# The second query up-projection tile and the transposes for the last residual, asked for at other places

## Chip, cores and metric

One NeuronCore of a Trainium2 chip runs the whole program. The metric is the device time of one execution in microseconds. A kernel is timed in several runs, and their median stands; one further execution is profiled.

## What is computed

Two transformer blocks over 256 tokens of width 1024, in float32. Two pieces of the reference matter here. In the first block's mixer, queries come out of a small projection:

```python
q = (rms_norm(c_q, g_cq) @ w_uq).reshape(B, L, MLA_HEADS, MLA_QK_DIM)   # 256 -> 8 heads x 96
q = rms_norm(q, g_q_mla)
```

In the second block, a layer of 16384 experts is added to the tokens h, and the result is normalised:

```python
u2 = rms_norm_2(h, norm2_g[l]) * (1 + sc2) + sh2
h = h + g2 * peer_layer(u2, peer_wq[l], peer_keys[l], peer_u[l], peer_v[l])
return rms_norm_2(h, final_g)
```

`peer_layer` projects the tokens to 8 heads of 2 x 128 queries, scores each half against 128 keys, chooses 16 pairs of keys for each head, and weighs expert activations.

## The kernel before

The work runs as one long stream of projections on TensorE. Tokens lie along the free dimension (256, with 16 meta tokens 272), features on the partitions, eight tiles of 128 for the width of 1024. A float32 product is made of three matmuls on rounded halves: high weight by high token, high by low, low by high (`mm3`, lines 118 to 121; a slice of 128 rows is three matmuls, a projection of 1024 rows 24).

**Weights.** `weights` (lines 89 to 108) loads one tile of 128 x 1024 on SP's queue (line 98), casts its high half on ScalarE (line 99, `whi`) and subtracts on VectorE, or on GpSimd where the call says so (line 100, `wlo`). Tiles of a name share buffers, given out in the order of use: three in the pool `w`, and in the first stages every fourth tile goes to a fourth buffer, `wx`. A cast can't start until the matmuls of the tile that had the buffer before are done.

**Order.** The program is written in plain Python order, and a planner sets the order of the instructions on each engine: the earliest in program order among what it believes ready. In `mixer` TensorE's order is the written one (`manual_schedule`), the other engines' is the planner's; in `experts` TensorE's is the planner's too. An engine works its list strictly in that order. SP's queue is such a list as well: a load that waits for a buffer holds up what stands behind it.

**Mixer, query up-projection** (lines 489 to 515). For each of two `w_uq` tiles g, four heads: six matmuls in a bank `sc`, a square on ScalarE (`qsq`), two multiplications on VectorE (`Q`, `qsw`). Behind a head follow a key's scaling (`scale_key`, from q = 2 on: two matmuls, then K's two multiplications on VectorE) and `step(1)`, half a projection of the `fq` or `fk` kind (`fox`): twelve matmuls. The second half of each calls `get_ready`, which requests the `w_in` tile of the next one. `fq` 0 to 3 use the `w_in` tiles 8 to 11; requests before are in this order: `w_in` 7, 8, `w_uq` 0, `w_in` 9, `w_in` 10, `w_uq` 1, `w_in` 11.

**Experts** (from line 1139). `raw` is the tokens times the gain, split in halves, slice k as soon as h[k] is final. Six query projections (line 1172, weights `peer_wq` 0 to 5) run on `raw` into six PSUM banks `mm`, while the sum of squares gives `r` (line 1178, in a bank `sc`, of which there are two, then a square root and a reciprocal). Then `affine` makes `u3` in eight slices (`aff` and `xl` on VectorE, `xh` on ScalarE) and `from_raw` (lines 781 to 788) multiplies a projection by `r` into `qt`, a tile named `pair`. `pair` has two buffers, shared by `qt` 0 and 1, the queries of later heads, and the transposed tokens. `scores` multiplies a head's queries with its keys in the banks `sc`. Projection 6 and later run on `u3`; projection 6 takes the bank of projection 0.

The tokens transposed, 16 transposes in four groups of four, each group in a bank `sc`, go through a copy (line 1165, to `pair`) and a store (line 1166) to `hd` in DRAM, which is read back near the end of the program. Once `h` is no longer read, its space goes to tiles of `experts`, the keys among them.

Of the kernel before, what the change touches and what calls it, by code (L numbers as in the profile page):

```python
# [10 lines left out]
F32 = mybir.dt.float32  # L11
# [12 lines left out]
S = 256  # L24
# [22 lines left out]
def two_blocks(ctx: ExitStack, tc: tile.TileContext, A, out):  # L47
    nc = tc.nc
    act, vec, pool, pe = nc.scalar, nc.vector, nc.gpsimd, nc.tensor
# [4 lines left out]
    ident = const.tile([128, 128], F32, name="ident")  # L54
# [5 lines left out]
    def col(name, k=0, p0=0, p1=128):  # L60
        o = COL[name][0] + k
        return cols[p0:p1, o:o + 1]

    xp = ctx.enter_context(tc.tile_pool(name="x", bufs=1))
    dram = ctx.enter_context(tc.tile_pool(name="hd", bufs=1, space=bass.MemoryType.DRAM))
# [18 lines left out]
    def bank(name):  # L84
        ids = banks[-1][name]
        ids.append(ids.pop(0))
        return ps.tile([128, 512], F32, name=name, tag=f"bank{ids[-1]}")
# [17 lines left out]
    def weights(*a, **kw):  # L105
        for w in weights_by_part(*a, **kw):
            pass
        return w
# [9 lines left out]
    def mm3(o, wh, wl, xh, xl, first, last):  # L118
        pe.matmul(o, lhsT=wh, rhs=xh, start=first, stop=False)  # L119
        pe.matmul(o, lhsT=wh, rhs=xl, start=False, stop=False)  # L120
        pe.matmul(o, lhsT=wl, rhs=xh, start=False, stop=last)  # L121
# [12 lines left out]
    def rstd_of(o, ssum, n):  # L134

        act.activation(o, ssum, AF.Sqrt, bias=eps[:o.shape[0]], scale=1.0 / n)
        vec.reciprocal(o, o)
# [36 lines left out]
    def split(p, x, T, nm, bufs=1):  # L174
        hi = p.tile([x.shape[0], T], F32R, name=nm + "h", bufs=bufs)
        lo = p.tile([x.shape[0], T], F32R, name=nm + "l", bufs=bufs)
        act.copy(hi, x)  # L177
        vec.tensor_sub(lo, x, hi)  # L178
        return hi, lo
# [4 lines left out]
    with psum(mm=8):  # L184
        o = bank("mm")
# [6 lines left out]
    for k in range(KC):  # L192
        if k % 4 < 2:
            first[k % 4] = next(loads[k % 4])
        t = hp.tile([128, T1], F32, name=f"h{k}")
# [60 lines left out]
    def mixer():  # L256
        es = ExitStack()
        p = es.enter_context(tc.tile_pool(name="mix", bufs=1))
# [48 lines left out]
        for c in range(2):  # L307
            t = p.tile([128, S], F32, name=f"cq{c}")
# [82 lines left out]
        for c in range(4):  # L391
            o = bank(("sc", "pm", "sc", "po")[c])
            cs = slice(c * 128, (c + 1) * 128)
            mm3(o[:, :T1], wkv[0][:, cs], wkv[1][:, cs], ckh, ckl, True, True)
            t = pw.tile([128, T1], F32, name="ksq", bufs=3)
# [12 lines left out]
        for i, t0 in enumerate((NM, NM + 128, 0)):  # L408
            o = bank("pm" if i == 1 else "sc")
            mm3(o, ckh[:, t0:t0 + 128], ckl[:, t0:t0 + 128], wkv[0][:, 512:], wkv[1][:, 512:], True, True)  # L410
            t = p.tile([128, 512], F32, name=f"V{i}")
# [73 lines left out]
        def sum_q(q0, q1):  # L485
            for q in range(q0, q1):
                pe.matmul(qsum[:8, :S], lhsT=sel[0:96, q], rhs=qsqs[q], start=False, stop=q == NH - 1)

        for g in range(2):
            wh, wl = weights(A["w_uq"][g])  # L490
            for q4 in range(4):
                q = 4 * g + q4
                o = bank("sc")
                for c in range(2):
                    cs = slice((q4 * 2 + c) * 128, (q4 * 2 + c + 1) * 128)
                    mm3(o[:, :S], wh[:, cs], wl[:, cs], cq3[c][0], cq3[c][1], c == 0, c == 1)
                t = pw.tile([96, S], F32, name="qsq", bufs=4)
                act.activation(t, o[0:96, :S], AF.Square)
                qsqs.append(t)
                qt = p.tile([96, S], F32, name=f"Q{q}")  # L500
                vec.scalar_tensor_tensor(qt, o[0:96, :S], col("gq", 0, 0, 96), rope[0:96, 0, NM:], op0=ALU.mult, op1=ALU.mult)
                t = pw.tile([96, S], F32, name="qsw")
                vec.scalar_tensor_tensor(t[64:96], o[96:128, :S], col("gq", 0, 96, 128), rope[96:128, 1, NM:], op0=ALU.mult, op1=ALU.mult)
                pool.tensor_add(qt[64:96], qt[64:96], t[64:96])
                Q.append(qt)
                if q == 1:
                    rfk = split(p, head_rstd(sum_fox("fk", T1), 64, T1, "rfk"), T1, "rfk")
                if q > 1:
                    scale_key(q - 2)
                step(1)  # L510
                if q > 4:
                    add_more(1)
                if q % 2 and q > 1:
                    sum_q(q - 3, q - 1)
# [164 lines left out]
        hx = [t[:, NM:] for t in h]  # L679
# [65 lines left out]
    def affine(p, xs, G, s0, r, T, nm, ks=range(KC)):  # L745

        res = []
        for k in ks:
            t = sm.tile([128, T], F32, name="aff")
            vec.scalar_tensor_tensor(t, xs[k], G[:, k:k + 1], r, op0=ALU.mult, op1=ALU.mult)  # L750
            hi = p.tile([128, T1], F32R, name=f"{nm}h{k}", bufs=1)[:, :T]
            lo = p.tile([128, T1], F32R, name=f"{nm}l{k}", bufs=1)[:, :T]
            sh = ada[:, s0 + k:s0 + k + 1]
            act.activation(hi, t, AF.Identity, bias=sh)
            vec.scalar_tensor_tensor(lo, t, sh, hi, op0=ALU.add, op1=ALU.subtract)  # L755
            res.append((hi, lo))
        return res
# [381 lines left out]
    def experts(hx):  # L1139
# [10 lines left out]
            return weights(ap, e=e, parts=parts, four=False, pin=pin)  # L1150

        qp = es.enter_context(tc.tile_pool(name="qp", bufs=2))
        qt = [qp.tile([128, 2, S], F32, name="pair") for n in range(2)]
        tc.keep_in_program_order(act.activation(dry, eps, AF.Sqrt))
        ss = sum_squares(sm, hx, S, vec)

        hd = dram.tile([128, 2, 1024], F32, name="hd")
        g2 = dram.tile([1, 1024], F32, name="g2")
        for i in range(2):
            for e2 in range(2):  # L1160
                o = bank("sc")
                for k in range(4):
                    pe.transpose(o[:, k * 128:(k + 1) * 128], hx[4 * e2 + k][:, i * 128:(i + 1) * 128], ident)
                t = qp.tile([128, 2, S], F32, name="pair").rearrange("p a b -> p (a b)")
                act.copy(t, o)
                nc.sync.dma_start(out=hd[:, i, e2 * 512:(e2 + 1) * 512], in_=t)
        vec.tensor_scalar(ada[:, 40:48], ada[:, 40:48], 1 / GATE, None, op0=ALU.mult)
        nc.sync.dma_start(out=g2.rearrange("a (k p) -> p (a k)", p=128), in_=ada[:, 40:48])
        G = gain_of(sm, 32, "norm2_g")
# [2 lines left out]
        for n in range(6):  # L1172
            o = bank("mm")
            project(o[:, :S + 2], wt(A["peer_wq"][n], vec if n == 1 else pool), raw, t1=S + 2)
            rp.append(o)
            if n == 0:
                o = bank("sc")
                tc.keep_in_program_order(pe.matmul(o[:, :S], lhsT=ones, rhs=ss, start=True, stop=True))
                r = qp.tile([128, S], F32, name="rstd", bufs=1)
                rstd_of(r, o[:, :S], 1024)  # L1180
        u3 = affine(xp, hx, G, 24, r, S, "x")
        rc = const.tile([128, 6], F32, name="rc")
        for n in range(4):
            from_raw(qt[n // 2][:, n % 2], rp[n], r, rc[:, n:n + 1])
# [2 lines left out]
        p = es.enter_context(tc.tile_pool(name="ex", bufs=1))  # L1187
# [178 lines left out]
        for m in range(KEYS // 2):  # L1366
# [10 lines left out]
            o = expert_acts(m, pool if m < OTHER else vec, OTHER <= m < DIRECT)  # L1377
            a = acts[:, 2 * m:2 * m + 2]
            if done:
                t = qp.tile([128, 2, S], F32, name="pair")  # L1380
# [43 lines left out]
        for i in range(2):  # L1424
            for n in range(3):
                add(ws[n], i, False, n == 2)
            for e2 in range(2):
                fs = slice(e2 * 512, (e2 + 1) * 512)
                t, x = part[:, 2 * i + e2], hf[:, i, fs]
# [13 lines left out]
    hx = [t[:, NM:] for t in h]  # L1443
# [147 lines left out]
```

## Time and profile before

| | us |
|---|---|
| median of 3 runs | 1692.92 |
| lowest and highest | 1692.71, 1694.39 |
| the profiled execution | 1697.36 |
| its span | 1695.6 |
| mean granted clock of TensorE in it | 0.99 |

The span is what the trace covers; the execution's time has 1.8 us more. Times in the trace are counted from the span's start. A matmul's start is recorded and its end is modelled, and matmuls overlap: intervals between starts tell the rate. PEclk is the share of full clock that was granted.

### The profile page before, as it was taken

To read this page: it belongs to the slowest core of one execution; us is meant where nothing else is said; L and a number is where in the kernel's file an instruction comes from. 1 tells how busy PE (TensorE), PEld (TensorE's weight loads), DVE (VectorE), ACT (ScalarE), POOL (GpSimd) and SP (SyncE) were. 2 spreads that over 40 slices of the span, in tenths; PEclk is the share of its full clock that TensorE was granted. 3 is DMA by queue.
4 is the path that set the end of the run, shared out by engine and by line. 5 is a ranking of instruction groups with operands and counts; after the bars stand their busy time and mean duration, and the time that the engine had idled before them with its cause. 6 is when DMAs were issued, how large, how long until landed. Compare 5 with 4: busy or idle time off the path is not lost.

```text
span 1695.6 us, 31038 instructions
## 1 busy us (share of the span) xinstructions
PE 1661.5 (98%) x11813; PEld 1539.0 (91%) x11813; DVE 1300.8 (77%) x2387; ACT 1015.3 (60%) x2037; POOL 133.4 (8%) x94
## 2 busy tenths in 40 slices
PE   9999999999999999999999989999999999999997
PEld 8999987799999888889989989999999988888886
DVE  8887677679875788886988997888889656666565
ACT  6544464664554776755664436988888555555554
POOL 3000002200000000000046920000000000000000
PEclk9999998999999999999999989999999999999999
DMA  7877642158786434336545545445454666655553
GB/s 264 287 235 251 204 149 88 38 199 275 259 265 177 160 133 141 134 113 209 177 155 171 175 138 173 161 163 169 164 165 162 194 232 196 195 191 198 189 197 125
DMA packets 90485, 308.20 MB, mean 182 GB/s; under 512 B 11352, under 2 KB 13912, under 8 KB 90208
## 3 DMA queue, kind: packets, MB, share of 16 engines
q1 hardware_dynamic: 90336, 306.22, 54.7%
q8 instruction: 93, 1.52, 0.4%
q14 instruction: 56, 0.46, 0.1%
HBM read 304.08 MB, written 2.10 MB: 181 GB/s over the span
## 4 chain that ended last, share of the span: by engine, by line
PE 85%; DVE 9%; ACT 4%; DMA 1%; issue 1%; SPq 0%; DVEq 0%; ACTq 0%
PE y L1407 20%; PE mm L119 17%; PE mm L121 17%; PE mm L120 17%; PE mm L824 5%; PE sc L1337 2%; DVE wlo L100 1%; ACT whi L99 1%; PE sc L548 1%; DMA wraw<-in_w_in_dram 1%; ACT tap L869 1%; DVE xl L755 1%; PE lev L978 1%; DVE acts L1252 1%; DVE acts L1250 0%
## 5 line engine op out<-in xcount | busy, mean ns | idle before, releaser
L99 ACT CAST whi<-wraw 128x1024 fp32r<-128x1024 f32 (+2 forms) x494 | 503.7, 1023 | 342.1 <-PE mm L120 230.7
L100 DVE TENSOR_TENSOR wlo<-wraw,whi 128x1024 fp32r<-128x1024 f32 (+2 forms) x457 | 545.3, 1197 | 202.7 <-ACT whi L99 199.9
L121 PE MATMUL mm<-xh,wlo 128*128 128x256 f32 (+1 forms) x2188 | 624.3, 285 | 10.6 <-DVE wlo L100 10.5
L119 PE MATMUL mm<-xh,whi 128*128 128x256 f32 (+1 forms) x2188 | 632.4, 289 | 1.7 <-ACT xh L169 1.1
L120 PE MATMUL mm<-xl,whi 128*128 128x256 f32 (+1 forms) x2188 | 620.4, 284 | 1.3 <-DVE xl L170 1.1
L121 PEld LDWEIGHTS mm<-xh,wlo 128*128 128x128 f32 x2188 | 415.5, 190 | 11.9 <-DVE wlo L100 11.8
L119 PEld LDWEIGHTS mm<-xh,whi 128*128 128x128 f32 x2188 | 416.6, 190 | 5.9 <-issue 3.1
L120 PEld LDWEIGHTS mm<-xl,whi 128*128 128x128 f32 x2188 | 416.9, 191 | 2.9 <-DVE xl L170 1.6
L1407 PE MATMUL y<-wlo,gah 128*128 128x512 f32 x512 | 158.0, 389 | 0.0
L1407 PE MATMUL y<-whi,gah 128*128 128x512 f32 x512 | 158.0, 389 | 0.0
L1407 PE MATMUL y<-whi,gal 128*128 128x512 f32 x512 | 157.6, 389 | 0.0
L177 ACT CAST gah<-acts 128x256 fp32r<-128x256 f32 x128 | 51.9, 407 | 146.6 <-PE y L1407 146.5
L1334 ACT ACTIVATE og<-oij,gtab 128x128 f16<-128x128 f16 x384 | 123.8, 394 | 19.7 <-DVE oij L1327 18.7
L824 PE MATMUL mm<-xw,wraw 128*128 128x256 f32 x560 | 131.2, 381 | 0.0
L100 POOL TENSOR_TENSOR wlo<-wraw,whi 128x1024 fp32r<-128x1024 f32 x37 | 92.5, 2508 | 342.4 <-ACT whi L99 339.1
L1407 PEld LDWEIGHTS y<-wlo,gah 128*128 128x128 f32 x512 | 96.1, 188 | 20.3 <-DVE wlo L100 0.4
L1407 PEld LDWEIGHTS y<-whi,gah 128*128 128x128 f32 x512 | 96.1, 188 | 20.3 <-ACT pair L1381 0.3
L1407 PEld LDWEIGHTS y<-whi,gal 128*128 128x128 f32 x512 | 96.1, 188 | 19.9
L824 PEld LDWEIGHTS mm<-xw,wraw 128*128 128x128 f32 x560 | 101.9, 190 | 13.1 <-issue 0.4
L178 DVE TENSOR_TENSOR gal<-acts,gah 128x256 fp32r<-128x256 f32 x128 | 54.1, 424 | 58.0 <-PE y L1407 58.0
L1327 DVE TENSOR_TENSOR oij<-iota,tab 128x1024 f16<-128x1024 f32 x64 | 77.7, 1218 | 1.4 <-PE sc L1337 1.3
L733 DVE CUSTOM_DVE_ANT_0 ada_w<-ada_w,silu_c 128x1024 f32<-128x1024 f32 x48 | 58.3, 1217 | 0.1
(904 smaller groups left out, 2351.4 us busy)
## 6 DMA issues: line engine op xcount, KB each, us to landing
wraw<-in_peer_u_dram SPq DMA_DIRECT2D x128, 512.0 KB, 3.3
wraw<-in_peer_v_dram SPq DMA_DIRECT2D x125, 512.0 KB, 3.3
wraw<-in_w_gu_dram SPq DMA_DIRECT2D x80, 512.0 KB, 4.6
wraw<-in_w_in_dram SPq DMA_DIRECT2D x80, 512.0 KB, 3.3
ada_w<-in_ada_w_dram SPq DMA_DIRECT2D x48, 512.0 KB, 4.9
wraw<-in_w_d_dram SPq DMA_DIRECT2D x32, 512.0 KB, 4.5
wraw<-in_w_out_dram SPq DMA_DIRECT2D x16, 512.0 KB, 3.8
wraw<-in_peer_wq_dram SPq DMA_DIRECT2D x16, 512.0 KB, 3.3
```

Of the source, the lines that this page charges most:

```text
L99: act.copy(hi[:, c], raw[:, c])
L100: sub = (e or vec).tensor_sub(lo[:, c], raw[:, c], hi[:, c])
L119: pe.matmul(o, lhsT=wh, rhs=xh, start=first, stop=False)
L120: pe.matmul(o, lhsT=wh, rhs=xl, start=False, stop=False)
L121: pe.matmul(o, lhsT=wl, rhs=xh, start=False, stop=last)
L177: act.copy(hi, x)
L178: vec.tensor_sub(lo, x, hi)
L733: tc.keep_in_program_order(vec.tensor_tensor_reduce(w, w, row, 1.0, 0.0, op0=ALU.mult, op1=ALU.add, accum_out=ada[:, g:g + 1]))
L824: pe.matmul(o, lhsT=w[:, k * 128:(k + 1) * 128], rhs=xw[k], start=k == 0, stop=k == KC - 1)
L1327: vec.tensor_tensor(out=oij, in0=iota[:, None, None, :].to_broadcast([128, 2, 4, 128]), in1=tab[:, :, ts][:, :, :, None].to_broadcast([128 ...
L1334: act.activation(og[:, part, k], oij[:, 1, k], AF.Copy, scale=gtab[:, part, 4 * t4 + k:4 * t4 + k + 1])
L1407: pe.matmul(y[i][e2], lhsT=x[:, ts], rhs=v[:, e2 * 512:(e2 + 1) * 512], start=first and n == 0, stop=last and n == 2)
```

## The change

`w_uq` 1 is requested ahead of head 2 instead of behind head 3, and so ahead of `w_in` 10 (`get_ready` in the step behind head 3). In `experts` the block of transposes, copies and stores stands behind the six query projections and the sum of squares' matmul, ahead of `affine`; the tiles `qt` are made behind it.

```diff
--- before.py
+++ after.py
@@ -486,10 +486,13 @@
             for q in range(q0, q1):
                 pe.matmul(qsum[:8, :S], lhsT=sel[0:96, q], rhs=qsqs[q], start=False, stop=q == NH - 1)
 
+        uq = [weights(A["w_uq"][0])]
         for g in range(2):
-            wh, wl = weights(A["w_uq"][g])
+            wh, wl = uq[g]
             for q4 in range(4):
                 q = 4 * g + q4
+                if q == 2:
+                    uq.append(weights(A["w_uq"][1]))
                 o = bank("sc")
                 for c in range(2):
                     cs = slice((q4 * 2 + c) * 128, (q4 * 2 + c + 1) * 128)
@@ -1150,20 +1153,9 @@
             return weights(ap, e=e, parts=parts, four=False, pin=pin)
 
         qp = es.enter_context(tc.tile_pool(name="qp", bufs=2))
-        qt = [qp.tile([128, 2, S], F32, name="pair") for n in range(2)]
         tc.keep_in_program_order(act.activation(dry, eps, AF.Sqrt))
         ss = sum_squares(sm, hx, S, vec)
-
-        hd = dram.tile([128, 2, 1024], F32, name="hd")
         g2 = dram.tile([1, 1024], F32, name="g2")
-        for i in range(2):
-            for e2 in range(2):
-                o = bank("sc")
-                for k in range(4):
-                    pe.transpose(o[:, k * 128:(k + 1) * 128], hx[4 * e2 + k][:, i * 128:(i + 1) * 128], ident)
-                t = qp.tile([128, 2, S], F32, name="pair").rearrange("p a b -> p (a b)")
-                act.copy(t, o)
-                nc.sync.dma_start(out=hd[:, i, e2 * 512:(e2 + 1) * 512], in_=t)
         vec.tensor_scalar(ada[:, 40:48], ada[:, 40:48], 1 / GATE, None, op0=ALU.mult)
         nc.sync.dma_start(out=g2.rearrange("a (k p) -> p (a k)", p=128), in_=ada[:, 40:48])
         G = gain_of(sm, 32, "norm2_g")
@@ -1178,7 +1170,18 @@
                 tc.keep_in_program_order(pe.matmul(o[:, :S], lhsT=ones, rhs=ss, start=True, stop=True))
                 r = qp.tile([128, S], F32, name="rstd", bufs=1)
                 rstd_of(r, o[:, :S], 1024)
+
+        hd = dram.tile([128, 2, 1024], F32, name="hd")
+        for i in range(2):
+            for e2 in range(2):
+                o = bank("sc")
+                for k in range(4):
+                    pe.transpose(o[:, k * 128:(k + 1) * 128], hx[4 * e2 + k][:, i * 128:(i + 1) * 128], ident)
+                t = qp.tile([128, 2, S], F32, name="pair").rearrange("p a b -> p (a b)")
+                act.copy(t, o)
+                nc.sync.dma_start(out=hd[:, i, e2 * 512:(e2 + 1) * 512], in_=t)
         u3 = affine(xp, hx, G, 24, r, S, "x")
+        qt = [qp.tile([128, 2, S], F32, name="pair") for n in range(2)]
         rc = const.tile([128, 6], F32, name="rc")
         for n in range(4):
             from_raw(qt[n // 2][:, n % 2], rp[n], r, rc[:, n:n + 1])
```

## Rows read from the trace of the kernel before

**Rows 1.** The page, part 1: busy time, share of the span, instructions.

```profile
PE 1661.5 (98%) x11813; PEld 1539.0 (91%) x11813; DVE 1300.8 (77%) x2387; ACT 1015.3 (60%) x2037; POOL 133.4 (8%) x94
```

**Rows 2.** Timeline of TensorE, five instructions behind idle time (start, us, operation).

```profile
260.51 0.41 PE L121 MATMUL sc<-cq0h,wlo 128*128 128x256 f32 x1 [3.05 <-DVE wlo L100]
...
580.59 0.38 PE L121 MATMUL mm<-xh,wlo 128*128 128x256 f32 x1 [1.16 <-DVE wlo L100]
...
870.42 0.70 PE L1178 MATMUL sc<-ss_acc,ones 128*128 128x256 f32 x2 [0.78 <-ACT pair L1165]
...
887.78 1.13 PE L1243 MATMUL sc<-keys,pair 128*128 128x128 f32 x8 [2.22 <-DMA keys<-in_peer_keys_dram]
...
998.72 0.58 PE L121 MATMUL mm<-xh,wlo 128*128 128x256 f32 x1 [8.27 <-DVE wlo L100]
```

**Rows 3.** Windows: length, busy PE, PEld, DVE, ACT, POOL; PEclk; DMA share, GB/s.

```profile
580.00:581.00 1.00, 0.41 (x3) 0.41 (x4) 1.00 (x3) 0.95 (x6) 0.00 (x0) 1.00 0.83 270
```

**Rows 4.** Timelines of VectorE, ScalarE and VectorE in the query up-projection.

```profile
244.69 1.20 DVE L100 TENSOR_TENSOR wlo<-wraw,whi 128x1024 fp32r<-128x1024 f32 x1
...
251.68 1.03 ACT L99 CAST whi<-wraw 128x1024 fp32r<-128x1024 f32 x1
...
258.43 0.43 DVE L469 TENSOR_TENSOR K<-rot,pt 32x272 f32<-32x272 f32 x1
...
259.24 2.35 DVE L100 TENSOR_TENSOR wlo<-wraw,whi 128x1024 fp32r<-128x1024 f32 x2
```

**Rows 5.** Busy time by stretch: the gap, and what follows it.

```profile
257.40:260.50 3.10, 0.06 (x1) 0.00 (x0) 2.99 (x7) 0.42 (x1) 0.72 (x1) 1.00 0.00 0
...
260.50:271.30 10.80, 10.79 (x42) 8.46 (x42) 6.86 (x12) 2.12 (x4) 2.08 (x3) 0.53 0.43 146
```

**Rows 6.** Timeline of TensorE, the transposes of line 1163.

```profile
864.12 0.93 PE L1163 MATMUL sc<-ident,h 128*128 128x128 f32 x7
...
866.56 1.04 PE L1163 MATMUL sc<-ident,h 128*128 128x128 f32 x8
```

**Rows 7.** Timeline of ScalarE, the copies; then landing of the stores, line 1166.

```profile
865.79 1.05 ACT L1165 COPY pair<-sc 128x512 f32<-128x512 f32 x2
...
869.79 0.58 ACT L1165 COPY pair<-sc 128x512 f32<-128x512 f32 x1 [2.54 <-DMA hd<-pair]
...
DMA to landing us min/median/max: 2.3/2.5/3.3
```

**Rows 8.** Timeline of TensorE at its low and its full clock.

```profile
263.20 0.41 PE L120 MATMUL mm<-xl,whi 128*128 128x256 f32 x1
...
264.48 0.41 PE L120 MATMUL mm<-xl,whi 128*128 128x256 f32 x1
...
271.70 0.28 PE L121 MATMUL sc<-cq0h,wlo 128*128 128x256 f32 x1
...
273.01 0.28 PE L121 MATMUL mm<-xh,wlo 128*128 128x256 f32 x1
...
273.72 0.28 PE L121 MATMUL mm<-xh,wlo 128*128 128x256 f32 x1
```

**Rows 9.** VectorE: sum of squares (timeline); line 755 (count, ns min/median/max, first, last start).

```profile
865.92 2.05 DVE L156 TENSOR_TENSOR ss_acc<-ss_acc,ss_sq 128x256 f32<-128x256 f32 x1 [0.55 <-ACT ss_sq L154]
...
L755 DVE SCALAR_TENSOR_TENSOR xl<-aff,ada,xh x8: 471/1316/2571, 875.3 to 887.8; 128x256 fp32r<-128x256 f32 x8
```

**Rows 10.** Timelines of VectorE, ScalarE and SP, early in `experts`.

```profile
874.80 0.41 DVE L787 TENSOR_TENSOR pair<-mm,rstd 128x256 f32<-128x256 f32 x1
...
885.98 1.98 ACT L99 CAST whi<-wraw 128x1024 fp32r<-128x1024 f32 x2
...
890.11 0.33 SPq L98 DMA_DIRECT2D wraw<-in_peer_wq_dram  x1
```

**Rows 11.** Timeline of TensorE behind the gap at 887.78.

```profile
890.88 2.08 PE L1243 MATMUL sc<-keys,pair 128*128 128x128 f32 x8 [1.11 <-ACT acts L1244]
...
895.52 0.32 PE L121 MATMUL mm<-xh,wlo 128*128 128x256 f32 x1
```

## Prediction

> **What bounds the kernel now.** I read the page first: TensorE is busy for 98% of the span [rows 1], so time can only come from the few places where it stands still or runs at the lower of its two clock levels (1.2 instead of 2.4 GHz). The timeline of TensorE, searched for idle time before an instruction, lists those places. Past the warming up at the start, only three gaps are followed by the low level: 3.05 us at 260.51, 2.22 us at 887.78, 8.27 us at 998.72 [rows 2]. A gap of 1.16 us at 580.59 is not: the granted clock stays at 1.00 there [rows 3]. Part one of the change aims at the first gap, part two at the stage that holds the second.
>
> In the query up-projection TensorE waits until 260.51 for a VectorE split, `wlo` of line 100, of the second `w_uq` tile. Its high half was cast at 251.68, when its buffer came free; its low half stands in VectorE's order behind K (and one `fq` instruction) and runs at 259.24 [rows 4]. VectorE has next to no idle time there (2.99 of 3.10 us busy); the stretch that follows, 260.5 to 271.3, has a mean granted clock of 0.53 [rows 5].
>
> At the start of `experts` the timelines read together: the 16 transposes stand half before, half behind the first eight matmuls of query projection 0; the sum of squares waits 0.78 us for the copy of the third transposed tile, because that copy waits 2.54 us for the first tile's store, both using the two `pair` buffers [rows 2, 6, 7]. The eight `xl` of `affine` start between 875.3 and 887.8 [rows 9]; TensorE has finished its six projections by 885.56 (887.78 - 2.22) and stands.
>
> **Part one, the weights.** Same instructions, other order: the second `w_uq` tile and the tile of `w_in` 10 change places in the ring of three weight buffers. `w_uq` 1 now takes the buffer and the slot in the queues that `w_in` 10 had (split at 244.69 [rows 4]): ready at 245.9, eleven us before head 4. That wait goes.
> What is late next is `w_in` 10 itself, needed by the third matmul of `fq` 2. It now needs the buffer that `w_in` 8 leaves (the cast at 251.68 was waiting for that one), and in program order its split stands after K's two multiplications and just before `fq` 1. VectorE is full until 258.86, so I put the split there: 258.86 + 1.2 = 260.06. The old wait cost 3.2 us (3.05 idle, and the 0.16 by which matmuls overlap otherwise), so the third matmul of head 4, which waited, now runs at 257.3. From there to the third of `fq` it is 1.31 us (271.70 to 273.01 in the next head at full clock [rows 8]): 258.6. So 1.5 us of wait stay, idle some 1.3, where 3.2 were lost: gain 1.7. Bounds for the new wait: 0, if the split slips in before K; 3.2, if it lands where the old one was.
> The clock: 1.3 us lies near 1.16, which kept the level, and below 2.22, which lost it; I take it as kept. Then 10.8 us at 0.213 us for a matmul become 6.0 at 0.119 [rows 8]: gain 4.8; if lost, about 0. VectorE must follow: of these 10.8 us it is busy for 6.86 [rows 5], idle for 3.9, a little less than the stretch is to shrink, so I take 0.5 off. Part one: -6.0 (bounds -8 to 0).
>
> **Part two, the transposes.** 16 transposes, 4 copies, 4 stores move behind six projections, on TensorE's, ScalarE's and SP's queues. TensorE's order here is the planner's: earliest in program order among what is ready. The timeline shows no hole in projections 1 to 5 (no idle row between 870.42 and 887.78 [rows 2]), their weights being split ahead, so I expect the transposes after the last of them.
> First the gain. Projection 0 starts at 864.12, where the first transpose stood [rows 6], but its last slice needs the low half of `raw` 7, which follows a sum of squares that runs beside a GpSimd split until 865.92 + 2.05 = 867.97 [rows 9]; with one instruction of 0.4 more, 868.4, and this doesn't move. TensorE waits about 1.4 us there, where transposes used to run (I take the clock as kept). The sum of squares' matmul then goes at 868.7 instead of 870.42, and projection 5 ends about 1.8 earlier, at 883.7.
> Then the price. `pair` has two buffers, and transposed tiles 0 to 3 come before `qt` 0 and 1 in the order of use, as before (the copies took both at 865.8, `qt` 0 was written at 874.80, after the third tile's store [rows 7, 10]). It can't be the other way round: `qt` would hold both until `scores(0)`, which needs the `sc` banks that hold the transposes. So `from_raw` of projection 0 now waits for transposes, copy, store, copy, store; and projection 6 needs the `mm` bank that this `from_raw` empties. All six banks are full: TensorE has nothing else. Nothing covers this.
> Shortest: 883.7 + 0.5 (four transposes) + 0.6 (copy) + 0.1 (issue) + 2.5 (store [rows 7]) + 0.6 + 0.1 + 2.5 + 0.4 (`from_raw`) + 0.5 for semaphores = 891.5. Longest likely: the first copy stands in ScalarE's order behind the last `xh` and the casts of projections 6 to 8, which ended at 887.96 [rows 10] and come about 1.5 earlier, so it starts at 886.4 instead of 884.3. Its store stands in SP's queue behind the load of `wq` 10, which waits for a GpSimd split (issued at 890.11 before [rows 10], 888.5 after): landing 891.4, copy and store of the third tile to 894.7, `from_raw` 895.2. I take 895.2, since SP's order follows from loads that are ready earlier in program order.
> By 895.5 before, the clock was back (the matmul at 895.52 is the last of more than 0.28 us) and TensorE had done 16 score matmuls (the second eight from 890.88) and 17 of projection 6 [rows 11]. From 895.2 these 33 take 33 x 0.214 = 7.1 us at the low level: 902.3, against 895.5: +6.8. From 891.5: +3.1. Later work is not in front of this: score matmuls and keys follow TensorE's projections, and the gap at 998.72 hangs on a VectorE chain that starts with the last of them, so all of it moves along. Part two: +6.8 (bounds -2, if no one waits for the transposes, to +9).
>
> A row and a rule on the same thing: `xl`, two SBUF inputs, takes 0.47 us at its shortest and up to 2.57, the long ones where a GpSimd split runs [rows 9]. The Trainium skill, SBUF — State Buffer, section "SBUF: two separate sides", says VectorE's and GpSimd's shared port pair is an exclusive lock held for a whole instruction. The 2.57 us agree. By that rule the chain to the last `xh` can't shrink to 16 short instructions and the copies stay late, +6.8; without it ScalarE would be free at 883.7 and the shorter price, +3.1, would hold.
>
> **Sum.** -6.0 + 6.8 = +0.8. The profiled execution took 1697.36 (span 1695.6 and 1.8 around it), 4.4 over the median of the runs, 1692.92; the difference carries over: 1698.2 profiled, 1693.7 as median.
>
> **Rivals.**
> *The wait at `w_in` 10 costs the clock too* (slower). One mechanism: the new gap before the third matmul of `fq` 2 is as good as the old one. It decides where the gap passes a length between 1.16 and 2.22 us. Part one then gives only 1.7 - 0.3: -1.4 + 6.8 = +5.4, 1698.3. For it: VectorE has no slack there. Chance 0.17.
> *The transposes cost nothing* (part two does not do what I say): the planner finds holes for them early, and the earlier reciprocal is a gain of about 2: -6.0 - 2 = -8.0, 1684.9. For it: before, they were cut in after eight matmuls; against: no holes among the projections. Chance 0.2.
> *The short chain*: copies and stores are not held up: -6.0 + 3.1 = -2.9, 1690.0. Against: the order of loads on SP. Chance 0.13.
> *My forecast*: 0.5, own range 1690.5 to 1698.
>
> **How the numbers follow.** Under 0.2% (3.4 us) a measurement can't tell a change of this kernel from none. Faster: nearly all of the second rival (0.19), not quite half of the third (0.06), 0.05 of the forecast: 0.30. Slower: 0.8 of the first rival (0.14) and 0.1 of the forecast's spread: 0.24. Same: 0.46. The range takes in the second rival's time and the first's: 1685 to 1699.
>
> **What would show it.** Right: no gap at head 4, a gap of 1 to 1.6 us before the third matmul of `fq` 2, granted clock 1.00 from 255 to 290; the 16 transposes after projection 5, then a gap of 6 to 10 us before projection 6, ending with `from_raw` after the third store; low clock after it. Wrong: transposes among the projections, `from_raw` near 873, or the low level near 260 as before. What would unsettle the sum most is another order from the planner ahead of the gap at 998.72, where TensorE waits for VectorE in both kernels.

## The result and the profile after

| | before | after |
|---|---|---|
| median of the runs, us | 1693.16 (1691.81 to 1696.89) | 1705.97 (1704.26 to 1707.03) |
| profiled execution, us (span) | 1697.36 (1695.6) | 1706.81 (1705.0) |

The ratio is 1.007, 95% interval 1.0058 to 1.0082: slower by 11.9 us (9.8 to 13.9). The ratio is taken over all six runs of each kernel, so its 11.9 is not the difference of the two medians (12.8). The forecast was no change, 1693.7 in a range of 1685 to 1699.

First, who kept TensorE waiting after the change: its longest waits by the line waited for (us in total, times, longest).

```profile
PE mm L121 <- DVE wlo L100: 13.6, 7, 8.3
...
PE mm L119 <- DVE pair L790: 9.2, 1, 9.2
...
PE sc L1179 <- ACT pair L1181: 4.2, 1, 4.2
...
PE sum L284 <- DVE rq_t L286: 1.5, 1, 1.5
```

The 3.05 us for `wlo` by an `sc` matmul at head 4 [rows 2] are gone. Two new lines hold 13.4 us: `from_raw` (`pair` of line 790, 9.2) and the copies of the transposed tiles (4.2). A third, `rq_t`, holds 1.5. The places, in TensorE's timeline after the change:

```profile
260.80 0.38 PE L121 MATMUL mm<-xh,wlo 128*128 128x256 f32 x1 [1.41 <-DVE wlo L100]
...
279.68 0.29 PE L284 MATMUL sum<-ident,fq_sum 8*128 8x8 f32 x2 [1.46 <-DVE rq_t L286]
...
579.70 0.38 PE L121 MATMUL mm<-xh,wlo 128*128 128x256 f32 x1 [1.17 <-DVE wlo L100]
...
882.62 1.04 PE L1179 MATMUL sc<-ident,h 128*128 128x128 f32 x8
...
887.84 1.97 PE L1179 MATMUL sc<-ident,h 128*128 128x128 f32 x8 [4.18 <-ACT pair L1181]
...
899.04 0.58 PE L119 MATMUL mm<-xh,whi 128*128 128x256 f32 x1 [9.23 <-DVE pair L790]
...
908.47 1.05 PE L1246 MATMUL sc<-keys,pair 128*128 128x128 f32 x8
...
1007.96 0.58 PE L121 MATMUL mm<-xh,wlo 128*128 128x256 f32 x1 [8.27 <-DVE wlo L100]
```

Three landmarks tell how far each stage moved, each a matmul behind a wait of the same length in both kernels. The one behind 1.16 us: 580.59 before [rows 2], 579.70 here. The one behind 8.27 us: 998.72 before, 1007.96 here, 9.24 later. Between them lies a third, 818.79 before and 817.66 here, 1.13 earlier, behind 0.60 us. So in this pair of executions part two cost 9.24 + 1.13 = 10.4 us. Part one brought 1.5: the trace of after starts 0.62 late (the matmul that waits 0.4 us for `fk` is at 231.16 against 230.54) and stands 0.89 early at 579.70.

The clock of the same trace, by windows (length; busy time of PE, PEld, DVE, ACT, POOL with counts; PEclk; DMA share; GB/s), answers to [rows 5]:

```profile
255.00:261.00 6.00, 4.59 (x28) 3.27 (x28) 5.75 (x12) 3.32 (x6) 1.45 (x2) 1.00 0.00 1
...
261.00:264.40 3.40, 3.40 (x17) 3.17 (x17) 3.17 (x6) 0.43 (x2) 0.72 (x1) 0.53 0.46 154
...
264.50:281.00 16.50, 14.58 (x89) 9.87 (x89) 14.50 (x26) 5.72 (x11) 9.74 (x11) 1.00 0.41 136
...
281.00:286.00 5.00, 5.00 (x23) 4.22 (x23) 2.33 (x15) 3.70 (x11) 1.49 (x2) 0.66 0.22 83
...
885.00:903.00 18.00, 5.92 (x27) 5.49 (x27) 3.72 (x16) 7.39 (x15) 4.65 (x2) 0.53 0.45 138
```

The level falls twice in the stretch of part one, behind the wait of 1.41 and behind the one of 1.46, for 3.4 us each. Before it fell once, for longer. At the transposes it is low for 17 us.

VectorE and GpSimd in the stretch of part one:

```profile
259.51 1.23 DVE L100 TENSOR_TENSOR wlo<-wraw,whi 128x1024 fp32r<-128x1024 f32 x1
...
273.80 3.09 DVE L100 TENSOR_TENSOR wlo<-wraw,whi 128x1024 fp32r<-128x1024 f32 x2
...
277.71 1.71 DVE L100 TENSOR_TENSOR wlo<-wraw,whi 128x1024 fp32r<-128x1024 f32 x1
...
279.45 0.17 DVE L286 COPY rq_t<-sum 128x16 f32<-128x16 f32 x1
...
274.30 8.27 POOL L449 TENSOR_TENSOR cum<-cum 8x272 f32<-8x272 f32 x7
```

The split of `w_in` 10 starts at 259.51, where the prediction put it. The copy of `rq_t` at 279.45, for which TensorE waits, comes straight behind the last of three more splits; two take 3.09 us together and one 1.71, where [rows 4] has 2.35 for two. GpSimd's seven additions run beside them.

And the chain of part two: two `xl` of `affine` on VectorE, ScalarE, SP's queue, the landing of the four stores (min, median, max), VectorE again:

```profile
877.80 4.84 DVE L758 SCALAR_TENSOR_TENSOR xl<-aff,ada,xh 128x256 fp32r<-128x256 f32 x2 [0.34 <-ACT xh L757]
...
885.34 1.98 ACT L99 CAST whi<-wraw 128x1024 fp32r<-128x1024 f32 x2
...
887.22 1.06 ACT L1181 COPY pair<-sc 128x512 f32<-128x512 f32 x2
...
894.90 1.07 ACT L1181 COPY pair<-sc 128x512 f32<-128x512 f32 x2 [6.62 <-DMA hd<-pair]
...
889.20 0.90 SPq L1182 DMA_DIRECT2D hd<-pair  x2
...
892.21 0.42 SPq L98 DMA_DIRECT2D wraw<-in_peer_wq_dram  x1
...
895.52 0.81 SPq L1182 DMA_DIRECT2D hd<-pair  x2
...
DMA to landing us min/median/max: 3.0/4.3/5.6
...
898.57 1.42 DVE L790 TENSOR_TENSOR pair<-mm,rstd 128x256 f32<-128x256 f32 x4 [12.55 <-DMA hd<-pair]
```

Copy at 887.22, store at 889.20, next copy at 894.90 when that store has landed, next store at 895.52, `from_raw` at 898.57. The chain is the one predicted, and it ends 4.5 us later than predicted.

### The profile page after: what moved, and what is told of

The parts are those of the page before. It is cut to its first block, busy times and chain, and to the rows that moved or that the text cites. A ratio compares the mean times of both kernels' runs of the same rounds, so it can differ in the third digit from the quotient of the medians.

```text
span 1705.0 us, 31041 instructions
## 1 busy us (share of the span) xinstructions
PE 1659.9 (97%) x11813; PEld 1537.8 (90%) x11813; DVE 1301.1 (76%) x2387; ACT 1016.7 (60%) x2037; POOL 134.8 (8%) x94
## 4 chain that ended last, share of the span: by engine, by line
PE 84%; DVE 8%; ACT 4%; issue 2%; DMA 1%; POOL 0%; SPq 0%; DVEq 0%; ACTq 0%; POOLq 0%
PE y L1410 20%; PE mm L119 17%; PE mm L121 17%; PE mm L120 16%; PE mm L827 5%; PE sc L1340 2%; DVE wlo L100 1%; PE sc L551 1%; DMA wraw<-in_w_in_dram 1%; ACT whi L99 1%; ACT tap L872 1%; PE lev L981 1%; DMA hd<-pair 1%; DVE acts L1255 1%; DVE acts L1253 0%
```

## Experiments

The indented paragraph of each experiment is what was expected before it ran. Several kernels share a stage with one of the two kernels, so a table of stages says more than whole times, which differ by up to 9 us between executions of one kernel (the kernel before: 1690.5 to 1699.3 in 29 of them). The mixer's stage is counted from the first matmul `pt<-rkh` (253.97 in the profile of before) to the one behind 1.16 us of wait (580.59); the experts' stage from the matmul behind 0.60 us (818.79) to the one behind 8.27 us (998.72). "Low" is the time at 1.2 GHz, summed over windows of 1 us, in 250 to 300 and in 860 to 920.

| kernel (profile) | mixer: stage, low | experts: stage, low |
|---|---|---|
| before | 326.6, 10.2 | 179.9, 6.8 |
| before, second profile (b1_before) | 323.6, 3.4 | 177.3, 0 |
| after | 325.1, 6.8 | 190.3, 17.1 |
| after, second profile (a1_after) | 325.0, 6.8 | 191.3, 17.1 |
| p1_weights | 322.0, 0 | 179.6, 6.8 |
| t1_transposes | 324.6, 6.8 | 191.2, 17.1 |
| t2_own4 | 323.7, 3.4 | 181.1, 6.8 |
| t4_before_own4 | 324.8, 6.8 | 178.7, 3.4 |
| t5_half_ring | 324.9, 6.8 | 187.5, 13.7 |
| t6_two_loads_less | 324.8, 6.8 | 190.0, 13.7 |
| t7_small_loads | 323.7, 3.4 | 188.2, 13.7 |
| p3_uq1_pool | 323.9, 6.8 | 177.3, 0 |
| p4_w14_15_pool | 323.8, 3.4 | 180.0, 6.8 |
| p6_pin15 | 323.6, 6.8 | 179.8, 6.8 |
| p8_w10_pool_pin15 | 319.2, 0 | 177.5, 0 |

### The parts alone: p1_weights, t1_transposes

```diff
# p1_weights: part one of the change on the kernel before
+uq = [weights(A["w_uq"][0])]
 for g in range(2):
-    wh, wl = weights(A["w_uq"][g])
+    wh, wl = uq[g]
...
+        if q == 2:
+            uq.append(weights(A["w_uq"][1]))
```

> Part one alone on the kernel before. Theory, from the trace of after: the head of 4.6 us that TensorE gains by the removed wait is given back to 1.5 us (1.46 us idle at 279.68 for a VectorE copy behind a split, and 1.6 us in a second low stretch from 282): 1691.7, and the same two gaps (1.41 near 260.8, 1.46 near 279.7) in its trace. Rival 1, the price on record: -6.0, 1687.2. Rival 2: the 3.4 us by which the medians differ more than the two traces belong to this part: 1695.1.

Measured: 1694.32 against 1695.38 for before in the same runs, ratio 0.9996 (0.9985 to 1.0008), that is -0.7 us (-2.5 to +1.4) by the ratio, which is used from here on. The two waits are there (1.41 at 260.91, 1.47 at 278.26). The price on record, -6.0, is excluded; -1.5 and no gain both fit. Rival 2, a loss hidden in this part, falls.

```diff
# t1_transposes: part two of the change on the kernel before
-qt = [qp.tile([128, 2, S], F32, name="pair") for n in range(2)]
-hd = dram.tile([128, 2, 1024], F32, name="hd")
-for i in range(2):
...
 # behind the loop over the six projections
+hd = dram.tile([128, 2, 1024], F32, name="hd")
+for i in range(2):
...
 u3 = affine(xp, hx, G, 24, r, S, "x")
+qt = [qp.tile([128, 2, S], F32, name="pair") for n in range(2)]
```

> Part two alone on the kernel before. Theory, from the trace of after: TensorE stands 4.2 us between the transposes and 9.2 us before projection 6, low clock after it: +10.3, 1703.5. Rival 1, the price on record: +6.8, 1700.0. Rival 2: both parts need each other for the loss, and part two alone costs under 3: below 1696.

Measured: 1707.72 against 1695.38, ratio 1.007 (1.0053 to 1.0087): +11.9 us (9.0 to 14.8). The same two waits, 4.19 and 9.17. The loss is all part two's, and more than the 6.8 on record. The two parts add up to the change, within their intervals (-0.7 + 11.9 against 11.9).

### Is it the ring? t2_own4, t5_half_ring, t4_before_own4

```diff
# t2_own4: part two, the transposed tiles in four buffers of their own
 qp = es.enter_context(tc.tile_pool(name="qp", bufs=2))
+own = ExitStack()
+tp = own.enter_context(tc.tile_pool(name="tp", bufs=4, side="right"))
...
-        t = qp.tile([128, 2, S], F32, name="pair").rearrange("p a b -> p (a b)")
+        t = tp.tile([128, 512], F32, name="turned")
...
+own.close()
 hs.close()
# t5_half_ring: bufs=2, tp for i == 0, the ring of `pair` for i == 1
# t4_before_own4: four buffers of their own, the transposes at their old place
```

> Part two alone, but the four transposed tiles have four buffers of their own, so that no copy waits for a store and the first queries' tiles wait for none of them. Theory (the ring of two buffers makes the 9.2 us): from_raw of projections 0 to 3 runs before 886, no gap of more than 3.5 us is left on TensorE between 880 and 905, and the time is that of before within 3 us, 1692. Rival (what costs is the place itself: TensorE's transposes wait for ScalarE's late copies, and stores stand behind the weights' loads on SP): projection 6 still starts after 893, 1699 or more.

Measured: ratio 1.0022 (1.0011 to 1.0033), +3.7 us instead of +11.9. VectorE's first `from_raw` (`pair` of line 787 there) and TensorE's two longest waits of the stretch:

```profile
872.29 0.41 DVE L787 TENSOR_TENSOR pair<-mm,rstd 128x256 f32<-128x256 f32 x1
...
882.46 0.38 PE L121 MATMUL mm<-xh,wlo 128*128 128x256 f32 x1 [1.41 <-POOL wlo L100]
...
892.99 1.17 PE L1246 MATMUL sc<-keys,pair 128*128 128x128 f32 x8 [2.65 <-DMA keys<-in_peer_keys_dram]
```

The first `from_raw` runs at 872.29, 13 us before the first store is issued (885.32), and projection 6 starts right behind the first eight transposes, at 880.57. The wait of 9.2 is gone, so the ring made it. Two waits are left. One is 2.65 us for the keys of the first scores, whose load stands behind the four stores on SP and is issued at 887.89. The other is 1.41 us in projection 6, for a split of GpSimd, with 3.4 us of low clock behind it. By the table the experts' stage is 2.3 us over the mean of the seven traces with the old order (178.8, t4 left aside); the rival is right as far as that. The theory's time, within 3 us of before, is neither met nor excluded: the interval is 1.9 to 5.6.

> Part two alone, with the first two transposed tiles in buffers of their own and the last two in the ring that the queries' tiles take over: the first queries wait for one store, not for two stores in a row. Theory (each link of the chain copy, store, copy, store costs its own time): from_raw of projection 0 near 895 instead of 898.6, TensorE's wait before projection 6 shorter by 3 to 4 us, the kernel 3.5 to 5.5 us faster than part two alone, some 1702. Rival (the four stores together take as long as two after two): from_raw at 898 or later, time as of part two alone.

Measured: 1704.48, ratio 1.0061 (1.0046 to 1.0076), that is +10.3 us where t1_transposes has +11.9. The medians differ by 3.2, but their runs stand beside other runs of before (medians 1693.72 and 1695.38), and the two intervals overlap, so the time alone shows no gain. The trace does:

```profile
896.36 0.58 PE L119 MATMUL mm<-xh,whi 128*128 128x256 f32 x1 [5.96 <-DVE pair L787]
...
DMA to landing us min/median/max: 4.7/4.8/5.1
```

The wait is 5.96 where it was 9.17: one copy and one store less in the row took away 3.2 us, though all four stores, now issued one behind the other, take 4.7 to 5.1 each. The forecast of the gap held (3 to 4), and the stage is 3.7 us shorter than in t1_transposes (187.5 against 191.2, with 13.7 us of low clock instead of 17.1). That the whole kernel gains 3.5 to 5.5 us is not shown.

> The kernel before, transposes at their old place, the four transposed tiles in four buffers of their own. Theory (the ring of two costs before only the 0.78 us at 870.42): no wait of a copy for a store, 0.5 to 2 us less than before. Rival (all four stores go out together ahead of the next weights and push them back): same as before or up to 3 us slower.

Measured: ratio 1.0008 (0.9997 to 1.0019). My theory falls: the 0.78 us of [rows 2] is gone and the wait for the keys grows from 2.2 to 4.50. What SP's load of the keys waited for, and VectorE:

```profile
SPq L1242 <- DVE aff L750: 2.3, 1, 2.3
...
878.66 4.87 DVE L755 SCALAR_TENSOR_TENSOR xl<-aff,ada,xh 128x256 fp32r<-128x256 f32 x2 [0.22 <-ACT xh L754]
```

The rival's time came, but not by its mechanism. The four stores are issued together by 867.94 and land in 2.7 to 3.4 us, long before. Counted from the landmark at 818.79 (818.08 here), TensorE is through its projections 1.0 us earlier, and the keys' load is issued 1.25 later: it waits for VectorE's last `aff`, which reads the `h` whose space goes to the keys, and which comes late behind the two `xl` above. Together these are the 2.3 us by which the wait grew.

### What stretches the stores: t6_two_loads_less, t7_small_loads

```diff
# t6_two_loads_less: part two alone
-project(o[:, :S], wt(A["peer_wq"][n], pool), u3, t1=S)
+if n not in (10, 11):
+    last[:] = [wt(A["peer_wq"][n], pool)]
+project(o[:, :S], last[0], u3, t1=S)
```

> Part two alone; the query projections 10 and 11 use the weights of projection 9 again, so their two loads of 512 KB, their casts and their splits are left out. Its whole time can't be compared; what is read is the stores. Theory (the first two stores take 5.6 us because two loads and the keys move at the same time): they land in 2.5 to 3.5 us, and TensorE's wait before projection 6 falls from 9.2 to 6 to 7 us. Rival (two stores of 256 KB at once, made of short rows, take that long by themselves): 5 us or more.

Measured: stores of 2.9 to 5.6 us, wait 9.72. This settles nothing: the buffers that were left free were taken by the next loads, and SP's queue shows the same issues as in the trace of after, at the same times to 0.1 us, up to 895.5. The traffic that I meant to take away was still there.

```diff
# t7_small_loads: the same transfers in the same order, two of them an eighth as large
-project(o[:, :S], wt(A["peer_wq"][n], pool), u3, t1=S)
+small = n in (10, 11)
+hi, lo = weights(A["peer_wq"][n], n=128 if small else 1024, e=pool, four=False)
+if small:
+    for k, (xh, xl) in enumerate(u3):
+        mm3(o[:, :S], hi[:, :128], lo[:, :128], xh[:, :S], xl[:, :S], k == 0, k == KC - 1)
+else:
+    project(o[:, :S], (hi, lo), u3, t1=S)
```

> Part two alone; the weights of the query projections 10 and 11 are loaded, cast and split in their first 128 of 1024 columns only (64 KB instead of 512), and these stand for all the others, so the result is another one; all transfers keep their order. What is read is the stores. Theory (the first two stores take 5.6 us because the loads next to them move at the same time): they land in 2.5 to 4 us, from_raw comes at 897 or before, and TensorE's wait before projection 6 is 1 to 3 us shorter than 9.2. Rival (two stores at once, with the keys, take that long by themselves): 5 us or more for the longest of them, wait as before.

TensorE's wait and the landing of the stores, in t1_transposes and then here:

```profile
899.59 0.58 PE L119 MATMUL mm<-xh,whi 128*128 128x256 f32 x1 [9.17 <-DVE pair L787]
...
DMA to landing us min/median/max: 2.8/4.2/5.7
...
895.03 0.58 PE L119 MATMUL mm<-xh,whi 128*128 128x256 f32 x1 [6.48 <-DVE pair L787]
...
DMA to landing us min/median/max: 2.4/2.7/3.7
```

The stores land in 2.4 to 3.7 us instead of 2.8 to 5.7 (t1_transposes), and the wait before projection 6 falls from 9.17 to 6.48. Traffic beside the stores is worth 2.7 us of the wait. The Trainium skill, DMA: Bandwidth & Descriptors, section "Issuing engines are not separate DMA queues", says that transfers run on the same 16 engines and interleave whoever issued them. In this stage SP issues all transfers, so these rows bear out one half of it: stores take longer beside loads.

### What part one turns into: p4, p3, p6, p8

Each of these changes who makes a low half, or when; p3 on the kernel before, the others on part one alone.

```diff
-ready.append(weights(A["w_in"][i]))
# p4_w14_15_pool
+ready.append(weights(A["w_in"][i], e=pool if i > 13 else vec))
# p6_pin15
+ready.append(weights(A["w_in"][i], pin=i == 15))
# p8_w10_pool_pin15
+ready.append(weights(A["w_in"][i], e=pool if i == 10 else vec, pin=i == 15))
# p3_uq1_pool, on the kernel before
-wh, wl = weights(A["w_uq"][g])
+wh, wl = weights(A["w_uq"][g], e=pool if g else vec)
```

> Part one alone, with the low halves of the w_in tiles 14 and 15 made by GpSimd, which takes the two splits out of VectorE's order ahead of the copy that TensorE waits for at 279.7. Theory (VectorE's order is what gives the gain back there): the gap of 1.46 goes and the clock stays at 1.00 from 265 on: 3.1 us below part one alone, 1688.6. Rival (VectorE is not the reason, or the two engines hold each other up): the gap stays or its place is taken, 1691.5 or more.

Measured: ratio 1.0004 (0.9992 to 1.0016). The rival. VectorE, GpSimd and TensorE in that trace:

```profile
276.58 0.18 DVE L286 COPY rq_t<-sum 128x16 f32<-128x16 f32 x1 [1.68 <-PE sum L284]
...
277.26 2.58 DVE L645 TENSOR_SCALAR rq_t<-rq_t 128x16 f32<-128x16 f32 x1
...
277.45 2.36 POOL L100 TENSOR_TENSOR wlo<-wraw,whi 128x1024 fp32r<-128x1024 f32 x1
...
281.68 0.94 PE L551 MATMUL sc<-K,Q 96*128 96x144 f32 x4 [1.48 <-DVE mn L558]
```

The copy of `rq_t` is on time (276.58), but the next small step of the same chain, 16 columns, takes 2.58 us, and ends 0.03 after GpSimd's split beside it. In the kernel after, beside the shorter additions, it took 0.17. That GpSimd's split held it is argued from the two ends; no run takes the split away and leaves the rest. TensorE waits 1.48 us a little later instead of 1.46. The Trainium skill, SBUF — State Buffer, section "SBUF: two separate sides", calls the port pair of the two engines an exclusive lock held for the whole instruction. For an instruction with one SBUF input, as this one, it says so of the two-port modes only. The length agrees; which mode ran no row shows, and which of the two came first, 0.19 us apart, these rows are too rough to tell.

> The kernel before, with the low half of the second w_uq tile made by GpSimd instead of VectorE; the ring of weights stays as it was. Cast at 251.7 and 2.4 us of GpSimd: ready near 256, so the wait of 3.05 us at head 4 goes without making the tile of w_in 10 late. Theory (VectorE bounds the whole stretch from 258 to 283): what TensorE gains is given back in waits for VectorE further on, time within 0.2% of before. Rival (the wait alone was the cost, as the prediction priced it): no gap over 0.5 us between 255 and 285, and 5 to 8 us less than before.

Measured: ratio 0.9993 (0.9982 to 1.0003), -1.2 us.

```profile
273.94 0.28 PE L284 MATMUL sum<-ident,q_sum 8*128 8x8 f32 x2 [0.45 <-ACT fq_sum L650]
...
276.40 0.38 PE L284 MATMUL sum<-ident,fq_sum 8*128 8x8 f32 x2 [1.84 <-DVE rq_t L286]
```

No wait at head 4, none at `w_in` 10, and TensorE still stands for 1.84 us at `rq_t`, with 6.8 us of low clock around it. The theory: the wait that the change aims at is not worth its price by itself, whichever way it is removed, because VectorE's order holds the end of the stretch.

> Part one alone, with VectorE's split of the w_in tile 15 held in program order, which puts it behind the copy of rq_t that TensorE waits for near 279; nothing else on VectorE moves. Theory (that split, 1.7 us beside GpSimd's adds, is what TensorE waits for): the gap of 1.46 is under 0.3, and the kernel is some 1.5 us under part one alone, up to 3 where the clock is kept too: ratio to before 0.998 to 0.999. Rival (VectorE is full whatever the order): the wait comes back within the next 25 us, at a VectorE result, and the ratio stays at 0.9996 within 0.001.

Measured: ratio 0.9982 (0.9972 to 0.9992), 2.4 us below part one alone by the ratios; the two intervals together leave that difference just short of clear. The trace is clear:

```profile
279.34 0.28 PE L284 MATMUL sum<-ident,q_sum 8*128 8x8 f32 x2 [0.45 <-ACT fq_sum L653]
...
279.66 0.17 DVE L286 COPY rq_t<-sum 128x16 f32<-128x16 f32 x1 [0.25 <-PE sum L284]
```

The copy now runs 0.32 us behind the first `sum` matmul, in the kernel after 1.85 (277.60 and 279.45). The wait at `rq_t` is gone and none takes its place before 578. The 1.41 at 261.03 stays, with 6.8 us of low clock behind it; with as much low time in all, the stage of after takes 325.1, this one 323.6. One split behind the copy instead of ahead of it is worth those 1.5 us in the trace: the theory.

> As the one before, and the w_in tile 10 split by GpSimd instead of VectorE, so that it is ready before the third matmul of fq 2. Theory (the two VectorE waits at 260.8 and 279.7 are all that part one left): no gap over 0.5 between 255 and 290, the clock at 1.00 there, and 4 to 7 us less than before, ratio 0.996 to 0.9977. Rival (VectorE bounds the stretch): the gap at 260.8 goes, but one of its length or more turns up before 300, ratio 0.9985 or above.

Measured: 1688.78 (1687.85 to 1689.56) against 1694.24, ratio 0.996 (0.9947 to 0.9973): 6.8 us faster than before (4.6 to 9.0): the theory. It is faster than both kernels. TensorE's only wait between 255 and 290, and the window:

```profile
274.73 0.28 PE L284 MATMUL sum<-ident,q_sum 8*128 8x8 f32 x2 [0.45 <-ACT fq_sum L653]
...
255.00:290.00 35.00, 34.38 (x227) 26.12 (x226) 30.94 (x85) 20.26 (x50) 13.08 (x16) 1.00 0.28 92
```

With both VectorE waits gone the clock is 1.00 throughout, and the mixer's stage is 319.2, 5.4 below the mean of the eight traces with the old mixer (324.6). That is the price on record for part one, at the cost of two more edits.

### How firm is the clock: b1_before, a1_after

Both kernels once more, with no edit.

> The kernel before once more, for a second profile. Theory (the low level after one and the same wait lasts differently from one execution to the next, which is what sets the spread of its times): TensorE's waits are those of the first profile within 0.3 us (3.05 at head 4, 8.27 before the first expert weights), but at least one of the low stretches, 10.2 us after head 4, 6.8 near 890, 10.2 near 995, has another length. Rival (the level follows the wait): the same lengths, and the difference of the times lies elsewhere.

The second profile of the kernel before, TensorE and two windows, to be set beside [rows 2, 5]:

```profile
260.32 0.38 PE L121 MATMUL sc<-cq0h,wlo 128*128 128x256 f32 x1 [3.05 <-DVE wlo L100]
...
883.60 1.13 PE L1243 MATMUL sc<-keys,pair 128*128 128x128 f32 x8 [2.19 <-DMA keys<-in_peer_keys_dram]
...
992.43 0.58 PE L121 MATMUL mm<-xh,wlo 128*128 128x256 f32 x1 [8.27 <-DVE wlo L100]
...
258.00:273.00 15.00, 12.68 (x76) 10.55 (x77) 12.42 (x22) 4.14 (x8) 4.00 (x6) 0.89 0.44 142
...
880.00:900.00 20.00, 16.27 (x137) 15.89 (x136) 19.66 (x100) 10.67 (x21) 14.53 (x6) 1.00 0.54 188
```

These three waits are the same to 0.03 us. The low level is not, as the theory said: the clock is 0.89 in 258 to 273 (3.4 us low) where the first profile has 10.2, and 1.00 in 880 to 900 where it has 6.8. The whole execution took 1691.36, 6 us less.

> The changed kernel once more, for a second profile. Theory: the same waits of TensorE within 0.3 us (1.41 near 261, 1.46 near 280, 4.2 and 9.2 after projection 5, 8.27 near 1008), with low stretches of other lengths than 3.4, 3.4, 17.1 and 10.2 us. Rival: waits differ too, so that the price of part two is not a fixed chain.

Measured: waits of 1.41, 1.47, 4.18, 9.37 and 8.27; the chain is fixed, as the theory says. That the low lengths would differ was wrong here: they are the same, 3.4, 3.4, 17.1 and 10.2. The execution took 1708.77, still 2.0 more than the first, of which 1.0 lies in the experts' stage: the low level is not all of the spread.

## Why the prediction was wrong, point by point

**The wait at head 4 goes and `w_in` 10 is late next: right.** Its split was put at 258.86 before `fq` 1 and ran at 259.51 - 0.62 = 258.89; the idle time was put at 1.3 and is 1.41. The gain of 1.7 in idle time is there.

**"I take it as kept", gain 4.8 from the clock: wrong, twice.** The wait of 1.41 before `w_in` 10 lost the level in three of its five traces (3.4 us in after and in its second profile, 6.8 in p6; 0 in p1 and p4), so a length between the 1.16 that kept it and the 2.22 that lost it decides nothing: the wait of 2.2 for the keys kept it in three of seven traces with the old order. And the 10.8 us at 0.53 were the longest case: after the same 3.05 the low level lasted 10.2, 6.8, 6.8, 6.8, 6.8, 3.4, 3.4, 3.4 us in eight executions, 6.0 on average. By the table's first column the stage of the old mixer takes 323.6 to 323.7 with 3.4 us low, 324.6 to 324.9 with 6.8 and 326.6 with 10.2.

**"VectorE must follow, I take 0.5 off": the other mis-sized term of part one.** [rows 5] ends at 271.3, where VectorE has 3.9 us free; the stretch in which it has none begins behind that, with three splits, K of the last heads and the `rq_t` chain. TensorE arrived there 4.6 us earlier (the first `sum` matmuls of the query sums at 277.60, before at 281.59, and 0.62 of late start), waited 1.46, and a second low stretch followed: of the 4.6 us, 3.1 were given back by 579.70, instead of 0.5. p3 shows it with the first wait removed in another way, p6 and p8 by moving one split behind the copy. The 4.6 itself is that large only in this pair, whose trace of before has the longest low stretch. Part one came to -0.7 (p1) instead of -6.0; with equal low time, 6.8 us, the mixer's stage is 325.0 to 325.1 after and 324.6 to 324.9 before.

**The order of part two: right.** Projection 5 was to end at 883.7; the transposes start at 882.62, which is 883.75 in the time of before. That it fits so closely is partly luck: the 1.4 us that TensorE was to wait in projection 0 came to 0.37, and 0.54 us for a GpSimd split (at 879.87) were not foreseen. Behind it stands the chain copy, store, copy, store, `from_raw`, and TensorE has nothing else, as said; t2 and t5 show that the ring of two buffers makes it. The gap ahead of 998.72 moved along unchanged (8.27 in both).

**The sizes of its terms: wrong, 5.1 us of the miss (+11.9 where +6.8 was forecast; part one's miss is 5.3).** In the time of after the first copy was to run at 886.4 - 1.1 = 885.3 and ran at 887.22, because ScalarE's last three `xh` wait for VectorE, which needs 4.84 us for two `xl` beside GpSimd's splits, and two casts follow. (This cause is read from the trace; no run tested it.) The first store was to land at 890.3 and landed at 894.9: issued 1.8 later, and 5.6 us long where 2.5 to 2.9 were taken from [rows 7], a stretch with less traffic. t7 gives 2.7 us of it back by making two loads small. From there the rest took 3.7 us, as priced. So `from_raw` was 4.5 late, TensorE started 0.5 behind it, and the catching up cost 1.4 less than 33 slow matmuls, because the low level ended at 902.9, 3.8 us after TensorE started, instead of lasting 7.1: 6.8 + 4.5 + 0.5 - 1.4 = 10.4, which is this pair of traces. Against the seven traces with the old order the stage is 12.1 longer (mean 190.9 of three against 178.8), in part because the first profile of before has 6.8 us of low clock in this stage and three of the seven have none, in part because the other two traces of the new order are 0.9 and 1.0 longer than that of after.

**The rivals.** The short chain is what t7 shows (wait 6.48), and its condition, copies and stores that are not held up, does not hold. Transposes that cost nothing: no; there was no hole for them. The clock lost at `w_in` 10: it was, in three of five traces, but its price was that of a stretch of 10.8 us (4.8); the stretch was of 3.4 or 6.8, and each 3.4 us of it cost the stage 1 to 2 us.

**The range** ended at 1699, the time of a rival. The upper ends of both parts, 0 and +9, were never put together (1702), and the +9 itself was too low, because the chain was priced with stores that nothing slows. With the parts as measured alone, -0.7 and +11.9, the sum is 11.2; the change measured 11.9.

**Left open.** Why t2_own4 is 3.7 us slower than before while its stage accounts for 2.3; the interval (1.9 to 5.6) holds both. Whether GpSimd's split beside the two `xl` is what made the first copy late. What sets the length of a low stretch after one and the same wait was not tried.

## What to carry to other kernels

Before a block that ends in a store is moved, look at whose buffers it shares: a ring of two makes the next users wait for a row of copies and landings, priced at the traffic of the new place and not of the old one. When a wait is removed, follow the engine that caused it to the end of its full stretch, not to the end of the slow clock; here one split behind a 16-column copy, and one on GpSimd, turned a gain that could not be told from nothing into 6.8 us. A gain that is to come from the clock needs several executions of the kernel before, since one profile shows only one length of the low stretch.

## What the runs showed of the chip that I had not expected

The same wait at the same place is followed by low stretches of 3.4, 6.8 or 10.2 us from one execution to the next, and by none or 6.8 at the keys. This goes with much of the spread of a kernel's times: the kernel before took 1691.36 with 3.4 us low at head 4 and none at the keys, 1697.36 with 10.2 and 6.8, and the two stages hold 5.6 of these 6 us. It isn't all: the two profiles of the kernel after have the same low stretches and differ by 2.0.

A VectorE instruction of 16 columns (line 645), 0.17 us long in the kernel after and 0.59 in p6, took 2.58 us beside one GpSimd subtraction of 2.36 us in p4. A split moved to GpSimd paid in p8, where nothing that TensorE waited for ran next to it, and not in p4.
